# Decoder block on one core: the second half of every block's low parts on GpSimd instead of VectorE

## The chip, the cores and the metric

The kernel runs on one core of a Trainium2 chip. Its engines work side by side, each through its own queue in order: TensorE (PE in the profile, its weight loads PEld), VectorE (DVE), ScalarE (ACT), GpSimd (POOL) and SyncE (SP), which issues the DMAs. They wait for each other through semaphores. The metric is the device time of one execution in microseconds (us), lower is better.

## The reference

One layer of a hybrid decoder over 256 tokens with a width of 2048. It is a chain of matrix products with large weights; everything is float32.

```
h = x + 1/2 * SwiGLU_1(RMSNorm(x))            # gate, up: 2048 x 5632, down: 5632 x 2048
proj = RMSNorm(h) @ W_in                      # 2048 x 7168: q f i g | B C v
o = gated linear recurrence(q, f, i), group norm, * silu(g)      # 8 heads of 128
y = B * causal conv3(C * v), group norm
h = h + concat(o, y) @ W_out                  # 2048 x 2048
h = h + 1/2 * SwiGLU_2(RMSNorm(h))            # as the first
h = h + sigmoid(RMSNorm(h) @ W_pg) * (p @ W_pe)
return RMSNorm(h)
```

## The kernel before, in words

All weights are read once, in blocks: a **step** (class `Step`) is one block of 16 (in every third step of a down projection, 12) square tiles of 128 x 128, and what is done with its product. There are 360 steps: twice 88 for gate and up, twice 48 for down, 72 in the mixer, 16 in the last stage. A token vector is the moving side of the product, 256 tokens wide.

To keep float32 accuracy with the faster float32r products, every operand is split in two: `hi` is the rounded value, `lo` what the rounding left. The activations lie as `xs[:, :T]` (high) and `xs[:, T:]` (low). A tile of weights then needs two matmuls in `product` (lines 104 to 109): `hi` against both halves, 512 columns, and `lo` against the high half, 256 columns.

The weights are split on the chip. `load` brings a block into one of 3 buffers `raw` by a DMA on SyncE's queue (line 85). `split` (line 98) takes a pair of `hi` and `lo` tiles for each half of the block, of 8 tiles or 1024 columns (768 in a block of 12), and calls `split_piece` for each half: ScalarE copies `raw` into `hi` with rounding (line 90), VectorE writes `lo = raw - hi` (line 91). `hi` and `lo` have 4 buffers each, so two blocks are held: the pair for a half of step i + 2 is free once TensorE is done with that half of step i. A `raw` buffer is free for the load of the block three steps on once both its halves are split.

The loop at the end of the kernel asks for the load three steps ahead and the split two steps ahead, then the step's products, its epilogue (VectorE and ScalarE take the sums out of PSUM, scale, gate, and write `hid` or `hT` and `xs`) and hooks, which in the mixer hold the recurrence's own work. A scheduler places the instructions of each engine by its own estimate of when each is ready, so that a queue's order isn't the program's order; only the start of the kernel (line 715 on) is written out by hand. There the first two blocks go side by side while x comes in, steps 2 and 3 are split, and VectorE sums the squares of x (lines 729 and 730) for the first `row_scale` (line 177), whose result the epilogues of the first steps use.

GpSimd does nothing before but fill a few constants: four tiny ones at the start and three memsets (lines 278 and 288) where the mixer opens.

Of the kernel before, what the change touches and what calls it, by code (L numbers as in the profile page):

```python
# [7 lines left out]
F32 = mybir.dt.float32  # L8
F32R = mybir.dt.float32r
I32 = mybir.dt.int32  # L10
AF = mybir.ActivationFunctionType
ALU = mybir.AluOpType
PSUM = bass.MemoryType.PSUM

P = 128
T = 256            # tokens
T2 = 2 * T
NB = 16            # 128-wide blocks of d_model
NF = 44            # 128-wide blocks of d_ff
NH = 8             # heads, conv groups  # L20
EPS = 1e-6
MAGIC = float(0x5F3759DF)
STAGES = (2, 8, 32)  # each joins four blocks of this many tokens
HW = 2 * NH        # heads x windows of 128 tokens
NM = 64 + 192 * len(STAGES)

# columns of the packed per-channel vectors
C_FFN1, C_MIX, C_FFN2, C_PLE, C_FIN = 0, 16, 32, 48, 64
C_HN, C_CN, C_CW, C_LB, C_SEL, C_ID = 80, 81, 89, 113, 129, 139
NCST = C_ID + P  # L30
# [4 lines left out]


class Step:
    """One block of at most 16 x [128, 128] weights and what is done with it."""

    def __init__(self, src, nk, mm, epi=None):  # L40
        self.src, self.nk, self.mm, self.epi = src, nk, mm, epi
# [5 lines left out]
def kernel(  # L47
# [3 lines left out]
    nc = tc.nc  # L51
    V, A, TE = nc.vector, nc.scalar, nc.tensor
# [5 lines left out]

    hT = const.tile([P, NB, T], F32, name="hT")
    xs = const.tile([P, NB, T2], F32R, name="xs")  # L60
    cst = const.tile([P, NCST], F32, name="cst")
    ones = const.tile([P, P], F32, name="ones")
    ones_r = const.tile([P, P], F32R, name="ones_r")
    sel = const.tile([P, 2 * P], F32R, name="sel")
    acc = const.tile([P, T], F32, name="acc")
    rb = const.tile([P, T], F32, name="rb")
    rt = const.tile([P, 2], F32, name="rt")
    lb = const.tile([P, NH], F32, name="lb")
    oml = const.tile([P, NH], F32, name="oml")
    ident = cst[:, C_ID:C_ID + P]  # L70

    def tt(shape=(P, T), dtype=F32, tag="t", bufs=6):
        return tmp.tile(list(shape), dtype, tag=tag, name=tag, bufs=bufs)

# [1 line left out]
    def new_raw(s):  # L76
        s.raw = wpool.tile([P, NB, P], F32, tag="raw", name="raw", bufs=RAW_BUFS)

    def new_parts(s):
        s.half = s.nk // 2  # L80
        s.parts = [tuple(wpool.tile([P, NB // 2, P], F32R, tag=t, name=t) for t in ("hi", "lo"))
                   for _ in range(2)]
# [4 lines left out]
    def split_piece(s, a, b):  # L87
        hi, lo = s.parts[a // s.half]
        r, sl = s.raw[:, a:b, :], slice(a % s.half, a % s.half + b - a)
        A.activation(hi[:, sl, :], r, AF.Copy)  # L90
        V.tensor_tensor(lo[:, sl, :], r, hi[:, sl, :].bitcast(F32), ALU.subtract)  # L91
# [4 lines left out]
            load_piece(s, i * s.nk // n, (i + 1) * s.nk // n)  # L96

    def split(s):
        new_parts(s)
        for k0 in (0, s.half):  # L100
            split_piece(s, k0, k0 + s.half)

    def product(hi, lo, m, ps, first, last):
        """ps[:, :T] += hi.x_hi; ps[:, T:] += hi.x_lo + lo.x_hi"""
        if not first:
            TE.matmul(ps[:, T:], lo, m[:, :T], start=False, stop=False)  # L106
        TE.matmul(ps, hi, m, start=first, stop=last)  # L107
        if first:
            TE.matmul(ps[:, T:], lo, m[:, :T], start=False, stop=False)  # L109

    def product_one(hi, lo, m, ps, first, last):
        """ps[:, :T] += all three"""
        TE.matmul(ps[:, :T], lo, m[:, :T], start=first, stop=False)  # L113
        TE.matmul(ps[:, :T], hi, m[:, T:], start=False, stop=False)  # L114
        TE.matmul(ps[:, :T], hi, m[:, :T], start=False, stop=last)  # L115
# [11 lines left out]
    def new_ps():  # L127
        return psum.tile([P, T2], F32, tag="ps", name="ps")

# [1 line left out]
    def halves(ps):  # L131
        t = tt()
        A.activation(t, ps[:, T:], AF.Copy)  # L133
# [41 lines left out]
    def row_scale():  # L175
        ps = new_ps()
        TE.matmul(ps[:, :T], ones, acc, start=True, stop=True)
        v = tt()
        V.tensor_scalar(v, ps[:, :T], 1.0 / (NB * P), EPS, ALU.mult, ALU.add)
        rsqrt(rb, v)  # L180
# [4 lines left out]
    def token_scale(ps):  # L185
        v = tt(shape=(P, 2), tag="v2", bufs=1)
        for i in range(2):
            V.tensor_scalar(v[:, i:i + 1], ps[i][:, 0:1], 1.0 / (NB * P), EPS, ALU.mult, ALU.add)
        rsqrt(rt, v)
# [11 lines left out]
        prep(j, c_gain)  # L201
        square_sum(j)

# [1 line left out]
    steps = []  # L205

    def at(i, f):
# [14 lines left out]
    def ffn(wg, wu, wd, c_next):  # L222
# [13 lines left out]
        i0 = len(steps)  # L236
        for f in range(NF):
            add(wg[f], NB, *gemm_in(g_epi))
            add(wu[f], NB, *gemm_in(u_epi(f)))

        def open_hid(s):
            st["pool"] = ExitStack()
            pool = st["pool"].enter_context(tc.tile_pool(name="hidp", bufs=1))
            st["hid"] = pool.tile([P, NF, T2], F32R, name="hid")

# [14 lines left out]
        steps[-1].after = close_hid  # L260
        return i0

# [1 line left out]
    def mixer():  # L264
        i0 = len(steps)
        m = {}
# [1 line left out]
        def open_mix(s):  # L268
            st["pool"] = ExitStack()
            m1 = st["pool"].enter_context(tc.tile_pool(name="mix1", bufs=1))  # L270
            m["Y"] = m1.tile([P, NH, T], F32, name="Y")
            m["Q"] = m1.tile([P, NH, T], F32, name="Q")
            m["masks"] = m1.tile([P, NM], F32, name="masks")
# [6 lines left out]
            m2 = st["hg"].enter_context(tc.tile_pool(name="mix2", bufs=1))  # L280
            m["K"] = m2.tile([P, NH, T], F32, name="K")
            m["f"] = m2.tile([P, NH * T], F32, name="f")
            m["t12"] = m2.tile([P, NH * T // 8], F32, name="t12")
            m["tot"] = [m2.tile([P, NH * T // n], F32, name=f"tot{n}") for n in (*STAGES, P)]
            m["V"] = m2.tile([P, 2, NH, P], F32, name="V")
# [49 lines left out]
                V.tensor_tensor(windows(m["Q"][:, h, :]), q_of(h), windows(f), ALU.mult)  # L335
            return epi

        # Tokens are taken in blocks whose length grows. Within a block Q holds q_t times the decays
        # from the block's start through t, K holds k_s times those after s to the block's end, tot
        # the whole block's: a score between two blocks is then a product of rows, no factor of which  # L340
        # exceeds 1, and the blocks between come in with their tot.
        def pairs(a):
            return a.rearrange("p (b two) -> p b two", two=2)

# [55 lines left out]
        def stage_scores(si, h):  # L400
            L = STAGES[si]
            nb = P // (4 * L)
# [44 lines left out]
            return d  # L447

        def stat(key, g, d, first, last):
            """rows g and NH + g: the sum over the group's channels"""  # L450
            if first:
                st[key] = new_ps()
            e = sel[:, P - g:2 * P - g]
            TE.matmul(st[key][:, :T], e, d[:, :T], start=first, stop=False)
            TE.matmul(st[key][:, :T], e, d[:, T:], start=False, stop=last)

        def stat_done(key):
            v = tt()
            V.tensor_scalar(v, st[key][:, :T], 1.0 / P, EPS, ALU.mult, ALU.add)
            r = tt()  # L460
            rsqrt(r, v)
            # rows g hold the high parts, rows NH + g the low ones
            rs = st["rs", key] = m["m1"].tile([P, T], F32R, tag="rs", name="rs", bufs=2)
            A.activation(rs, r, AF.Copy)
            V.tensor_scalar(r, r, cst[:, C_SEL + 9:C_SEL + 10], None, ALU.mult)
            V.scalar_tensor_tensor(rs, rs.bitcast(F32), cst[:, C_SEL + 8:C_SEL + 9], r, ALU.mult, ALU.add)
# [4 lines left out]
            st["nr" + key, g] = d  # L471

        def norm(key, g, t):
            """t (in place) times its group's scale"""
            ps = new_ps()
            TE.matmul(ps[:, :T], ones_r, st["nr" + key, g], start=True, stop=True)
            V.tensor_tensor(t, ps[:, :T], t, ALU.mult)
# [45 lines left out]
        g0 = len(steps)  # L523
# [14 lines left out]
        k = c0 + 3  # L538
# [25 lines left out]
        for h in range(NH):  # L564
            at(k + 2 + h // 2, lambda h=h: norm_rows("o", h))
            at(k + 3 + h // 2, lambda h=h: norm("o", h, m["Q"][:, h, :]))
        assert k + 3 < g0  # a head's norm comes before its gate

        def conv_out(key, c):
            y = m["Y"][:, c, :]  # L570
# [3 lines left out]
        for c in range(NH):  # L574
            key = "y0" if c < 4 else "y1"
# [20 lines left out]
        steps[-1].after = close_mix  # L596
        return i0

# [1 line left out]
    def ple():  # L600
        i0 = len(steps)
        m = st["ple"] = {}
# [84 lines left out]
    scale_at = {i_f1 + 4, i_mix, i_f2, i_ple}  # L687
    late = []

# [1 line left out]
    # the first gate and up blocks side by side, so that both go on while x comes in  # L691
    nc.sync.dma_start(cst, cst_d)
    for i in range(2):
        steps[i].src = w_first[i]
# [17 lines left out]
    with tc.manual_schedule():  # L712
        for a, b in pieces:
            s = steps[a // 8]
# [15 lines left out]
        V.tensor_tensor(acc, acc, rb, ALU.add)  # L730

    def prologue():
        # the lower bound of the forget gate: the softmax's first row
        mx, e0, e1 = (tt(shape=(P, NH), tag="lbt", bufs=3) for _ in range(3))
        l0, l1 = cst[:, C_LB:C_LB + NH], cst[:, C_LB + NH:C_LB + 2 * NH]
        V.tensor_tensor(mx, l0, l1, ALU.max)
        V.tensor_tensor(e0, l0, mx, ALU.subtract)
        V.tensor_tensor(e1, l1, mx, ALU.subtract)
        A.activation(e0, e0, AF.Exp)
        A.activation(e1, e1, AF.Exp)  # L740
        V.tensor_tensor(e1, e0, e1, ALU.add)
        V.reciprocal(e1, e1)
        V.tensor_tensor(lb, e0, e1, ALU.mult)
        V.tensor_scalar(oml, lb, -1.0, 1.0, ALU.mult, ALU.add)
# [23 lines left out]
        if s.after:  # L768
            s.after(s)

# [1 line left out]
    m = st["ple"]  # L772
    ps = st["ts"]
    token_scale(ps)
# [3 lines left out]
    ps = new_ps()  # L778
# [66 lines left out]
```

## Time and profile before

| | |
|---|---|
| time of two runs | 2048.87 and 2050.26 us, median 2049.57 us |
| the profiled execution | span 2047.5 us from first to last instruction; the page gives no other time of its own |
| TensorE (matmuls) | 2028.2 us busy, 99% of the span |
| VectorE | 1373.2 us, 67% |
| ScalarE | 1004.2 us, 49% |
| GpSimd | 2.9 us, 7 instructions |
| DMA | 374 MB read, 184 GB/s over the span |
| chain that ended last | 98% of it matmuls |

The busy share alone doesn't tell what a faster or slower engine would change: the chain of waits tells which engine the end is tied to, the list of waits tells who stands idle for whom, and the timeline shows by how much an instruction is early for the one that needs it.

### The profile page before, as it was taken

The page shows a single profiled execution, that of the slowest core. Times are in us where ns is not written, and L with a number is a line of the kernel's source. Part 1 is how long each engine was busy: PE and PEld are TensorE (multiplying, and loading weights), DVE is VectorE, ACT ScalarE, POOL GpSimd, SP SyncE. Part 2 cuts the span into 40 slices and gives each one's busy share as a digit, 9 for nine tenths or more (in the row PEclk, how much of TensorE's full clock was granted, in tenths as well). Part 3 has the DMA queues.
Part 4 walks back from the last instruction along what each step waited for, and adds up shares of the span by engine and source line. Part 5 has one row for each costly group of instructions (what it writes and reads, how often), then busy time and mean ns, then how long its engine had stood idle before and what let it go on. Part 6 is the DMA issues. An engine that isn't in the chain of part 4 may idle for free.

```text
span 2047.5 us, 29112 instructions
## 1 busy us (share of the span) xinstructions
PE 2028.2 (99%) x11630; PEld 1774.8 (87%) x11630; DVE 1373.2 (67%) x2131; ACT 1004.2 (49%) x1510; POOL 2.9 (0%) x7
## 2 busy tenths in 40 slices
PE   8999999999999999999999999999999999999997
PEld 7888888888888888888888888888888888888986
DVE  8766666666555565689798776666666665555686
ACT  7444444444444444543566544444444444444463
POOL 0000000000000000000000000000000000000000
PEclk9999999999999999999999999999999999999998
DMA  7555555555555555544455555555555555555642
GB/s 250 205 188 188 191 193 188 186 185 182 184 190 190 185 199 190 189 165 145 144 168 186 187 185 192 192 188 185 185 186 187 190 186 188 177 195 187 237 164 84
DMA packets 55720, 378.00 MB, mean 185 GB/s; under 512 B 6176, under 2 KB 6432, under 8 KB 13728
## 3 DMA queue, kind: packets, MB, share of 16 engines
q1 hardware_dynamic: 55584, 376.14, 53.8%
q8 instruction: 91, 1.49, 0.3%
q14 instruction: 45, 0.37, 0.1%
HBM read 374.02 MB, written 2.10 MB: 184 GB/s over the span
## 4 chain that ended last, share of the span: by engine, by line
PE 98%; DMA 1%; DVE 1%; SPq 0%; issue 0%; ACT 0%; DVEq 0%; ACTq 0%
PE ps L107 61%; PE ps L106 29%; PE ps L109 2%; PE ps L405 1%; PE ps L306 1%; PE ps L307 1%; PE ps L308 1%; PE ps L114 1%; PE ps L115 1%; PE ps L113 1%; DMA hT<-xT 0%; DMA raw<-w1g 0%; PE ps L352 0%; DVE hg L782 0%; PE ps L438 0%
## 5 line engine op out<-in xcount | busy, mean ns | idle before, releaser
L107 PE MATMUL ps<-xs,hi 128*128 128x512 f32 x3824 | 1330.7, 394 | 5.9 <-DVE xs L154 5.9
L91 DVE TENSOR_TENSOR lo<-raw,hi 128x1024 fp32r<-128x1024 f32 (+2 forms) x724 | 865.1, 1195 | 637.4 <-ACT hi L90 636.6
L90 ACT ACTIVATE hi<-raw 128x1024 fp32r<-128x1024 f32 (+2 forms) x724 | 750.2, 1037 | 981.3 <-PE ps L107 624.2
L106 PE MATMUL ps<-xs,lo 128*128 128x256 f32 x3585 | 1002.3, 280 | 0.3 <-DVE lo L91 0.3
L107 PEld LDWEIGHTS ps<-xs,hi 128*128 128x128 f32 x3824 | 704.4, 188 | 156.2 <-ACT hi L90 5.9
L106 PEld LDWEIGHTS ps<-xs,lo 128*128 128x128 f32 x3585 | 672.3, 188 | 11.6 <-DVE lo L91 0.8
L107 PE MATMUL ps<-hid,hi 128*128 128x512 f32 x1320 | 461.3, 393 | 0.0
L106 PE MATMUL ps<-hid,lo 128*128 128x256 f32 x1290 | 364.5, 283 | 0.0
L107 PEld LDWEIGHTS ps<-hid,hi 128*128 128x128 f32 x1320 | 245.9, 188 | 54.8
L106 PEld LDWEIGHTS ps<-hid,lo 128*128 128x128 f32 x1290 | 242.5, 188 | 1.5
L140 DVE TENSOR_TENSOR t<-t,rb 128x256 f32<-128x256 f32 x231 | 97.5, 424 | 6.6
L134 DVE TENSOR_TENSOR t<-ps,t 128x256 f32<-128x256 f32 x239 | 99.8, 418 | 0.2 <-ACT t L133 0.2
L133 ACT ACTIVATE t<-ps 128x256 f32<-128x256 f32 x239 | 87.1, 366 | 0.9 <-DVE rb L162 0.9
L107 PE MATMUL ps<-mixout,hi 128*128 128x512 f32 x240 | 83.6, 397 | 0.0
L109 PE MATMUL ps<-xs,lo 128*128 128x256 f32 x239 | 67.8, 284 | 0.1
L106 PE MATMUL ps<-mixout,lo 128*128 128x256 f32 x225 | 63.1, 281 | 0.0
L109 PEld LDWEIGHTS ps<-xs,lo 128*128 128x128 f32 x239 | 45.1, 189 | 10.1 <-DVE lo L91 1.0
L107 PEld LDWEIGHTS ps<-mixout,hi 128*128 128x128 f32 x240 | 44.1, 188 | 9.5
L145 ACT ACTIVATE s<-t 128x256 f32<-128x256 f32 x112 | 45.0, 402 | 0.6 <-DVE t L140 0.6
L106 PEld LDWEIGHTS ps<-mixout,lo 128*128 128x128 f32 x225 | 42.2, 188 | 0.9 <-ACT mixout L149 0.2
L232 DVE TENSOR_TENSOR t<-t 128x256 f32<-128x256 f32 x88 | 37.3, 424 | 2.9
L150 DVE TENSOR_TENSOR hid<-t,hid 128x256 fp32r<-128x256 f32 x88 | 36.7, 418 | 0.1
(177 smaller groups left out, 931.9 us busy)
## 6 DMA issues: line engine op xcount, KB each, us to landing
raw<-w_in SPq DMA_DIRECT2D x48, 1024.0 KB, 4.9
raw<-w2g SPq DMA_DIRECT2D x44, 1024.0 KB, 4.8
raw<-w2u SPq DMA_DIRECT2D x44, 1024.0 KB, 4.8
raw<-w1u SPq DMA_DIRECT2D x43, 1024.0 KB, 4.8
raw<-w1g SPq DMA_DIRECT2D x42, 1024.0 KB, 4.8
raw<-w1d SPq DMA_DIRECT2D x32, 1024.0 KB, 4.9
raw<-w2d SPq DMA_DIRECT2D x32, 1024.0 KB, 4.9
raw<-w_out SPq DMA_DIRECT2D x16, 1024.0 KB, 4.8
```

The costliest lines, as they stand in the source:

```text
L90: A.activation(hi[:, sl, :], r, AF.Copy)
L91: V.tensor_tensor(lo[:, sl, :], r, hi[:, sl, :].bitcast(F32), ALU.subtract)
L106: TE.matmul(ps[:, T:], lo, m[:, :T], start=False, stop=False)
L107: TE.matmul(ps, hi, m, start=first, stop=last)
L109: TE.matmul(ps[:, T:], lo, m[:, :T], start=False, stop=False)
L113: TE.matmul(ps[:, :T], lo, m[:, :T], start=first, stop=False)
L133: A.activation(t, ps[:, T:], AF.Copy)
L134: V.tensor_tensor(t, ps[:, :T], t, ALU.add)
L140: V.tensor_tensor(dst, t, rb, ALU.mult)
L145: A.activation(s, src, AF.Sigmoid)
L150: V.tensor_tensor(dst[:, T:], src, dst[:, :T].bitcast(F32), ALU.subtract)
L232: V.tensor_tensor(u, u, st["g"], ALU.mult)
```

## The change

`split` no longer calls `split_piece` for the second half of a block. ScalarE writes `hi` of that half as before, and the subtraction that writes `lo` is issued on GpSimd, with the same operands and shape. It holds for the 358 blocks that go through `split`; the first two blocks, which are split in pieces by hand, stay as they were. Comment lines were dropped and `split` is longer, so that line numbers behind it are 4 higher than before.

```diff
     def split(s):
+
         new_parts(s)
-        for k0 in (0, s.half):
-            split_piece(s, k0, k0 + s.half)
+        split_piece(s, 0, s.half)
+        hi, lo = s.parts[1]
+        r = s.raw[:, s.half:s.nk, :]
+        A.activation(hi[:, :s.half, :], r, AF.Copy)
+        nc.gpsimd.tensor_tensor(lo[:, :s.half, :], r, hi[:, :s.half, :].bitcast(F32), ALU.subtract)
```

The scheduler answers with other orders. At the start of the kernel, on TensorE, around the matmul that sums the squares over the partitions (`ps<-acc,ones`, of `row_scale`), before:

```order
L107 MATMUL ps<-xs,hi 128x512
L106 MATMUL ps<-xs,lo 128x256
L107 MATMUL ps<-xs,hi 128x512
L177 MATMUL ps<-acc,ones 128x256
L107 MATMUL ps<-xs,hi 128x512
L109 MATMUL ps<-xs,lo 128x256
```

and with the change:

```order
L110 MATMUL ps<-xs,lo 128x256
L111 MATMUL ps<-xs,hi 128x512 x2
L181 MATMUL ps<-acc,ones 128x256
L113 MATMUL ps<-xs,lo 128x256
L110 MATMUL ps<-xs,lo 128x256
L111 MATMUL ps<-xs,hi 128x512
```

Before, it stood at the end of step 4; now it stands behind the first matmul of step 4, 31 matmuls earlier.

On VectorE at the same place, the sums of squares (`acc<-acc,t` and `rb<-rb,t` by turns, then `acc<-acc,rb`) and the low parts around them, before:

```order
L91 TENSOR_TENSOR lo<-raw,hi 128x1024 x4
L729 TENSOR_TENSOR acc<-acc,t 128x256
L729 TENSOR_TENSOR rb<-rb,t 128x256
...
L91 TENSOR_TENSOR lo<-raw,hi 128x1024
L730 TENSOR_TENSOR acc<-acc,rb 128x256
L91 TENSOR_TENSOR lo<-raw,hi 128x1024 x4
L179 TENSOR_SCALAR t<-ps 128x256
```

and with the change:

```order
L91 TENSOR_TENSOR lo<-raw,hi 128x1024 x2
L733 TENSOR_TENSOR acc<-acc,t 128x256
L733 TENSOR_TENSOR rb<-rb,t 128x256
...
L734 TENSOR_TENSOR acc<-acc,rb 128x256
L91 TENSOR_TENSOR lo<-raw,hi 128x1024
L183 TENSOR_SCALAR t<-ps 128x256
```

The low parts of the second halves are gone from VectorE's queue, and that of step 4's first half now stands behind the sum `acc<-acc,rb`.

On GpSimd, where the mixer opens, the memsets stood alone; now they stand among the low parts (`ub` and `S` are tiles of the mixer):

```order
L105 TENSOR_TENSOR lo<-raw,hi 128x768
L105 TENSOR_TENSOR lo<-raw,hi 128x1024
L282 MEMSET ub_6748 128x2
L282 MEMSET ub_6749 128x2
L292 MEMSET S 128x3072
L105 TENSOR_TENSOR lo<-raw,hi 128x1024 x161
```

The low parts behind the memsets wait in the queue until these are done. SyncE's queue holds the same loads in the same order; each now waits for GpSimd as well as for VectorE.

## Rows read from the trace of the kernel before

**Rows 1.** The page: span; busy us by engine; chain that ended last.

```profile
span 2047.5 us, 29112 instructions
...
PE 2028.2 (99%) x11630; PEld 1774.8 (87%) x11630; DVE 1373.2 (67%) x2131; ACT 1004.2 (49%) x1510; POOL 2.9 (0%) x7
...
PE 98%; DMA 1%; DVE 1%; SPq 0%; issue 0%; ACT 0%; DVEq 0%; ACTq 0%
```

**Rows 2.** Waits: who stood idle for whom, total, times, longest in us.

```profile
DVE lo L91 <- ACT hi L90: 636.6, 647, 2.8
...
PE ps L107 <- DVE xs L154: 5.9, 1, 5.9
```

**Rows 3.** Groups by line and shape: count, busy us, mean ns, idle before.

```profile
L91 DVE TENSOR_TENSOR lo<-raw,hi 128x1024 fp32r<-128x1024 f32 x652 | 798.3, 1225 | 581.8 <-ACT hi L90 581.4
L91 DVE TENSOR_TENSOR lo<-raw,hi 128x768 fp32r<-128x768 f32 x64 | 61.3, 958 | 54.6 <-ACT hi L90 54.4
```

**Rows 4.** Timeline, gate and up: start us, us, engine, line, idle before.

```profile
301.09 0.28 PE L109 MATMUL ps<-xs,lo 128*128 128x256 f32 x1
...
301.11 1.06 ACT L90 ACTIVATE hi<-raw 128x1024 fp32r<-128x1024 f32 x1 [1.45 <-PE ps L107]
...
302.21 1.23 DVE L91 TENSOR_TENSOR lo<-raw,hi 128x1024 fp32r<-128x1024 f32 x1 [1.25 <-ACT hi L90]
...
303.46 0.33 SPq L85 DMA_DIRECT2D raw<-w1g  x1
...
303.91 1.06 ACT L90 ACTIVATE hi<-raw 128x1024 fp32r<-128x1024 f32 x1 [1.47 <-issue]
...
306.69 0.28 PE L109 MATMUL ps<-xs,lo 128*128 128x256 f32 x1
```

**Rows 5.** DMA issues: count, KB each, median us from issue to landing.

```profile
raw<-w1u SPq DMA_DIRECT2D x43, 1024.0 KB, 4.8
```

**Rows 6.** Timeline of GpSimd where the mixer opens.

```profile
750.25 2.67 POOL L288 MEMSET S<- 128x3072 f32 x1
```

**Rows 7.** Busy time by stretch: gate and up; the recurrence in the mixer.

```profile
200.00:400.00 200.00, 200.00 (x1143) 174.45 (x1142) 133.77 (x197) 96.51 (x143) 0.00 (x0) 1.00 0.55 187
890.00:985.00 95.00, 94.81 (x559) 85.50 (x558) 90.40 (x196) 41.39 (x56) 0.00 (x0) 1.00 0.43 145
```

**Rows 8.** The same stretches, VectorE's line 91 alone.

```profile
200.00:400.00 200.00, 87.00 (x71) 1.00 0.55 187
890.00:985.00 95.00, 31.27 (x26) 1.00 0.43 145
```

**Rows 9.** Timeline at the start: the split of steps 2 to 4.

```profile
19.11 1.06 ACT L90 ACTIVATE hi<-raw 128x1024 fp32r<-128x1024 f32 x1 [0.21 <-DMA raw<-w1g]
21.59 2.01 ACT L90 ACTIVATE hi<-raw 128x1024 fp32r<-128x1024 f32 x2 [1.42 <-DMA raw<-w1u]
...
28.42 4.13 ACT L90 ACTIVATE hi<-raw 128x1024 fp32r<-128x1024 f32 x4
```

**Rows 10.** Timeline at the start, VectorE: the last sums of squares.

```profile
29.60 0.41 DVE L729 TENSOR_TENSOR rb<-rb,t 128x256 f32<-128x256 f32 x1
...
31.07 0.41 DVE L730 TENSOR_TENSOR acc<-acc,rb 128x256 f32<-128x256 f32 x1
```

**Rows 11.** Timeline at the start, TensorE: steps 2, 4 and 5.

```profile
22.89 0.28 PE L106 MATMUL ps<-xs,lo 128*128 128x256 f32 x1
...
31.07 0.62 PE L107 MATMUL ps<-xs,hi 128*128 128x512 f32 x2
31.53 0.28 PE L109 MATMUL ps<-xs,lo 128*128 128x256 f32 x1
...
36.90 0.59 PE L177 MATMUL ps<-acc,ones 128*128 128x256 f32 x2
37.14 0.58 PE L107 MATMUL ps<-xs,hi 128*128 128x512 f32 x1
```

**Rows 12.** Timeline of the recurrence, TensorE: score products behind VectorE's update `K`.

```profile
963.82 2.84 PE L405 MATMUL ps<-M,K 128*128 128x192 f32 x16 [0.20 <-DVE K L424]
```

## The prediction

> **What bounds the kernel now.** I read the chain that ended last first: 98% of it are matmuls [rows 1], so the end is tied to TensorE and time is won or lost only where TensorE waits. The list of waits comes next: the one long wait of TensorE is 5.9 us, for the first `xs` at the start, while VectorE stands idle for 636.6 us before its low parts [rows 2]. The reader is to see there that the split has time to spare and TensorE, 2028.2 us busy, has not [rows 1]. Last the timeline of one step in gate and up [rows 4]: step to step is 306.69 - 301.09 = 5.60 us, and half a step 2.80 us.
>
> **What is removed.** `split` issues 2 x 358 low parts: 652 of 1024 columns and 64 of 768 [rows 3]. Half of them leave VectorE: 326 x 1.225 + 32 x 0.958 = 430 us of VectorE's time, 21% of the span. On the path that sets the end this is worth nothing. VectorE's low parts had idle time before them nearly everywhere (636.6 us in total [rows 2]), and no matmul of the steady part waits for one. What covers it is TensorE itself, so no gain is booked.
>
> **What is added, and its price.** 358 subtractions on GpSimd. The trace has no GpSimd operation that reads anything. The nearest row is the memset of 3072 columns in 2.67 us [rows 6]: 0.87 ns a column, 0.89 us for 1024 columns, for one stream that is written. That is the lower bound. The subtraction has three streams, two read and one written; one after the other at the memset's rate they take 3 x 0.89 = 2.67 us. I take this value, as it stands on the only row of the same engine. For the upper bound I let each operation also wait out all that VectorE still does in a step: (133.77 - 87.00 / 2) / (200 / 5.60) = 2.53 us [rows 7, 8], so 2.67 + 2.53 = 5.20 us.
>
> [...]
>
> **What covers the new operation in the steady part.** The ScalarE copy at 301.11 starts right as a step ends, so it refills the second half's buffers of the step just done, for use two steps on [rows 4]. The first matmul on that half comes at 306.69 + 2.80 = 309.5. GpSimd can start where VectorE did, at 302.2: it has 7.3 us, and even 5.20 us fits. The second condition is spacing: one such operation a step, so it must take under 5.60 us. The third is the load: SyncE issues the next load at 303.46, as soon as the second half's low part is done [rows 4]. It lands 4.8 us later [rows 5], at 308.3. That buffer belongs to the block three steps on, whose first half is read two steps after the copy at 303.91, at 315.1, so the load may be 6.8 us later. GpSimd delays it by 2.67 - 1.23 = 1.4 us, or 4.0 us at the upper bound. SyncE's queue holds only loads in the same order here, each equally early. ScalarE's queue has nothing that waits for GpSimd. Cost in the steady part: 0 us.
>
> **GpSimd's queue where the mixer opens.** Its low part stands behind the memsets, which wait for the end of the down projection and are done at 750.25 + 2.67 = 752.9 [rows 6]. It is needed a step and a half after that end, about 8.40 us after 750.2, at 758.6. With 2.67 us it is done at 755.6, with 5.20 at 758.1. Cost 0 us.
>
> **The start.** Here the cover is thin. (a) Step 2's second half: its high part is ready at 19.11 + 1.06 = 20.17 [rows 9]; plus 2.67 it is done at 22.84, and TensorE's matmul with it starts at 22.89 [rows 11]. At 5.20 us it would be 2.5 us late. (b) The sum over the partitions moves one step forward, from 36.90 to just behind the pair at 31.07, some 31.3 [rows 11]. Its input is ready when VectorE's sums end: 29.60 + 0.41 = 30.0 [rows 10], then the last addition, 30.4. The low part of step 4's first half now stands behind it and ends at some 31.6; TensorE wants it at 31.53 plus the 37.14 - 36.90 = 0.24 of the moved matmul, 31.77. So there is 0.2 us to spare. GpSimd's operation for step 3 starts at 21.59 + 2.01 = 23.6 [rows 9], just as the sums begin. If it held them up for its whole 2.67 us, TensorE would wait 2.5 us; if that of step 4, ready at about 30.5, did so too, 5.2 us. I take half of the first, 1.3 us, with 0 and 5.2 as ends.
>
> **Sum.** -0 + 0 + 0 + 1.3 us. The profiled execution has a span of 2047.5 us [rows 1]; the runs are 2048.87 and 2050.26 us, 1.4 to 2.8 us lie around the span, and the median is 2.1 us above it. 2047.5 + 2.1 + 1.3 = **2051 us**. The likeliest case alone runs from 2047.5 (no cost, and two microseconds less than the median for orders that happen to fall better) to 2055 (both delays at the start).
>
> **Rival 1: VectorE and GpSimd hold each other up.** A VectorE operation that reads two tiles from SBUF and the new GpSimd one may not run side by side. Against it speaks nothing in the trace, since GpSimd reads nothing there. In gate and up it would still fit: 2.53 + 2.67 = 5.20 of 5.60 us. In the recurrence it wouldn't: VectorE is busy 90.40 of 95 us [rows 7]. It gives away 13 of its 26 low parts, 15.6 us [rows 8], and takes on 13 x 2.67 = 34.7: 109.5 us for 95, 14.5 over. TensorE has nothing to spare there: its score products at 963.82 already waited 0.20 us for the update `K` [rows 12]. With 2.5 to 5.2 us at the start: 2049.6 + 3.9 + 14.5 = 2068 us, between 2055 and 2075. For less speaks that copies out of PSUM and operations with one tile need not be held up.
>
> [...] I keep the forecast ahead, since queues that slip by a microsecond or two find 5 us of cover almost everywhere.
>
> **Rival 2, the other side: GpSimd becomes the bound.** If the spacing of its operations passes 5.60 us, TensorE waits in every step. Alone, an operation would have to take over 5.60 us, 6.3 times the memset's rate; if it is held up by all that VectorE does, over 5.60 - 2.53 = 3.07 us suffice. At 4.0 us, held up: 176 steps of gate and up x 0.93 = 164 us, in the recurrence 14.5 + 13 x 1.33 = 32, at the start 5: 2250 us. The memset's rate speaks against it; that no row shows a subtraction there, speaks for it.
>
> **Rival 3: nothing changes,** because the scheduler leaves the work where it was. The order of GpSimd's queue shows the subtractions there, so I give it next to nothing. Faster by over 2% would need 41 us off a TensorE that is idle for 2047.5 - 2028.2 = 19.3 us in all [rows 1]; the end of the kernel has no split in it.
>
> **Chances.** Forecast 0.63, rival 1 0.21, rival 2 0.14, nothing or a gain 0.02. The range takes the forecast's own range and rival 1 up to its upper end: 2047 to 2075 us, with about 0.81 in it; left out is mainly rival 2. Under 2% either way is about what a measurement here can tell from no change: 41 us. Forecast and rival 1 both lie inside it: same 0.85, slower 0.14, faster 0.01.
>
> **What the profile after should show.** Line 105 on GpSimd x358, near 2.7 us; VectorE some 940 us busy; TensorE's share at 99%, and no long wait for GpSimd's `lo`; small waits, if any, between 20 and 35 us. Rival 1 would show VectorE's operations of two inputs longer than before while GpSimd runs, and waits of the score products in the recurrence. Rival 2 would show GpSimd over 90% busy and TensorE waiting for it in every step. The forecast is wrong if the span moves by more than 8 us, or if the waits at the start are not where the microseconds go.

## The result, and the profile after

The changed kernel takes **2075.3 us** (median of 2073.87 and 2076.72), against 2049.57 before: a ratio of 1.0126, 95% interval 1.0096 to 1.0155. That is 1.3% slower, clear of the noise, though inside the 2% that count as no change. The forecast was 2051 us, the range ended at 2075, and rival 1 stood at 2068.

The page of the kernel after: span, busy us by engine, and the chain that ended last.

```profile
span 2072.1 us, 29503 instructions
...
PE 2037.0 (98%) x11630; PEld 1776.4 (86%) x11630; DVE 1482.1 (72%) x1773; ACT 989.4 (48%) x1510; POOL 866.7 (42%) x365
...
PE 84%; DVE 11%; ACT 3%; issue 2%; DMA 1%; POOL 0%; SPq 0%; DVEq 0%; ACTq 0%; POOLq 0%
```

Against [rows 1] TensorE stands idle for 2072.1 - 2037.0 = 35.1 us instead of 19.3, and the chain now has 11% of VectorE in it. VectorE gave away 430 us of work and is busy for 109 us *more*. So its remaining instructions became longer. The groups of the kernel after, by line and shape (count, busy us, mean ns, idle before), say which:

```profile
L144 DVE TENSOR_TENSOR t<-t,rb 128x256 f32<-128x256 f32 x231 | 424.1, 1837 | 6.9
...
L203 DVE TENSOR_TENSOR t<-hT,t 128x256 f32<-128x256 f32 x45 | 111.4, 2476 | 31.5 <-ACT t L202 31.5
L138 DVE TENSOR_TENSOR t<-ps,t 128x256 f32<-128x256 f32 x239 | 101.1, 423 | 50.7 <-ACT t L137 47.6
...
L105 POOL TENSOR_TENSOR lo<-raw,hi 128x1024 fp32r<-128x1024 f32 x326 | 803.6, 2465 | 1081.5 <-ACT hi L104 1081.5
```

`t<-t,rb` and `t<-hT,t` read two tiles in SBUF. In the kernel before they took 424 and 419 ns:

```profile
L140 DVE TENSOR_TENSOR t<-t,rb 128x256 f32<-128x256 f32 x231 | 97.5, 424 | 6.6
...
L199 DVE TENSOR_TENSOR t<-hT,t 128x256 f32<-128x256 f32 x45 | 18.9, 419 | 0.0
```

Line 138 has the same shape but reads one operand from PSUM, and still takes 423 ns. The low part that stayed on VectorE went from 1225 ns [rows 3] to 1276 only: it runs almost wholly before GpSimd starts. Line 105 is the new operation, 2.47 us.

The waits of the kernel after (total, times, longest in us) show that TensorE waits for GpSimd's low part only a few times, and briefly:

```profile
ACT s L149 <- DVE t L144: 280.7, 109, 4.5
...
PE ps L409 <- DVE K L428: 3.7, 2, 2.0
...
PE ps L113 <- POOL lo L105: 1.5, 7, 0.2
```

ScalarE waits for the long `t<-t,rb` 109 times, 280.7 us in all. TensorE waits for VectorE's update `K` and, 2.7 us in all, for `nr`, an operand of the mixer's norms; it waits seven times for a low part of GpSimd's, all in the output projection (below).

**Where the 24.6 us are,** the difference of the two spans. I set the start of the first weight matmul of a step in a later trace against that of the same step before; the difference is how late the step is. The matmuls of the changed kernel come in the same order as before but for nine. Late, in us:

| step (before at) | what lies behind it | changed kernel | GpSimd writes only | sums in PSUM | only in the mixer | two of 512 columns |
|---|---|---|---|---|---|---|
| 10 (65.38) | the start | 3.27 | 1.32 | 3.49 | -0.02 | 3.78 |
| 160 (885.42) | gate, up, down, mixer's projections | 3.27 | 0.82 | 3.00 | -0.02 | 3.78 |
| 184 (1053.34) | the recurrence, the first norms | 10.16 | 0.41 | 11.25 | 12.01 | 6.82 |
| 200 (1144.41) | the mixer's last norm, the opening of the output projection | 18.32 | 0.58 | 14.88 | 20.09 | 10.63 |
| 209 (1195.39) | the rest of the output projection, one step more | 24.21 | 0.57 | 14.88 | 24.10 | 10.63 |
| 359 (2026.36) | the second feed-forward part, the last stage | 24.21 | 0.58 | 14.88 | 24.10 | 10.63 |

So the changed kernel loses 3.3 us at the start, 6.9 in the recurrence, 8.2 from the last norm to the opening of the output projection, 5.9 from there on, and nothing from step 10 to 160 and from step 209 on. In the recurrence the update `K` itself is no longer than before; operations ahead of it in VectorE's queue are (`M<-Q,tot`, two tiles of SBUF, 1418 ns on the mean instead of 687). (The other columns belong to the experiments below. In those of writing only and of 512 columns, 1.8 and 2.6 us were there already as step 2 opened, before GpSimd's first low part; 0.2 in the changed kernel.)

**Gate and up: held, and yet free.** The timeline of the kernel after (start us, us, engine, line, idle before) at the place of [rows 4]:

```profile
299.92 2.46 POOL L105 TENSOR_TENSOR lo<-raw,hi 128x1024 fp32r<-128x1024 f32 x1 [3.21 <-ACT hi L104]
...
300.60 2.06 DVE L144 TENSOR_TENSOR t<-t,rb 128x256 f32<-128x256 f32 x1
...
302.69 0.42 ACT L149 ACTIVATE s<-t 128x256 f32<-128x256 f32 x1 [2.58 <-DVE t L144]
...
304.38 1.06 ACT L104 ACTIVATE hi<-raw 128x1024 fp32r<-128x1024 f32 x1 [0.33 <-PE ps L111]
...
305.52 2.40 POOL L105 TENSOR_TENSOR lo<-raw,hi 128x1024 fp32r<-128x1024 f32 x1 [3.15 <-ACT hi L104]
```

GpSimd ends at 299.92 + 2.46 = 302.38, VectorE at 300.60 + 2.06 = 302.66, 0.28 us later: it stood until GpSimd was done, then finished. The sigmoid `s` on ScalarE waited 2.58 us for it, and behind the sigmoid in the same queue stands the next copy `hi`, which releases GpSimd's next operation. That is a ring: `hi`, GpSimd, held `t*rb`, sigmoid, next `hi`. Here it still closes in time: the last copy waited 0.33 us for TensorE's release of the buffer (the copy of every second step does), so the ring is shorter than two steps by that much, and the spacing is 305.52 - 299.92 = 5.60 us as before. As the ring keeps pace with the steps, GpSimd's low part is still done some 4.6 us before TensorE comes to the half that needs it.

**Output projection: the same ring, too long.** The timeline of the kernel before, two copies `hi` one step apart:

```profile
1161.53 1.06 ACT L90 ACTIVATE hi<-raw 128x1024 fp32r<-128x1024 f32 x1 [1.01 <-PE ps L107]
...
1167.17 1.06 ACT L90 ACTIVATE hi<-raw 128x1024 fp32r<-128x1024 f32 x1 [1.01 <-PE ps L107]
```

A step takes 1167.17 - 1161.53 = 5.64 us, and the copy waits for TensorE. The kernel after:

```profile
1178.09 1.04 ACT L104 ACTIVATE hi<-raw 128x1024 fp32r<-128x1024 f32 x1
...
1179.21 2.50 POOL L105 TENSOR_TENSOR lo<-raw,hi 128x1024 fp32r<-128x1024 f32 x1 [3.65 <-ACT hi L104]
...
1179.43 2.56 DVE L203 TENSOR_TENSOR t<-hT,t 128x256 f32<-128x256 f32 x1
...
1181.76 0.38 PE L113 MATMUL ps<-mixout,lo 128*128 128x256 f32 x1 [0.23 <-POOL lo L105]
...
1182.56 0.51 ACT L157 ACTIVATE xs<-hT,cst 128x256 fp32r<-128x256 f32 x1 [3.16 <-DVE hT L204]
...
1184.23 1.05 ACT L104 ACTIVATE hi<-raw 128x1024 fp32r<-128x1024 f32 x1
```

From `hi` to `hi` it is 1184.23 - 1178.09 = 6.14 us. The held addition ends 0.28 us behind GpSimd again (1181.99 and 1181.71), and ScalarE stands 3.16 us before `xs`, with no idle time before its copies. So the ring sets 6.14 us, and each of GpSimd's low parts comes 0.5 us later against its step than the one before. The projection also multiplies the second halves of its blocks first (`order`), so that GpSimd's low part is needed as a step opens and not half a step later. Up to step 199 it still comes in time; from step 200 on TensorE waits for it (at 1181.76, just behind GpSimd's end). Seven steps lose 0.5 us each and the last 0.7; the other 1.7 are lost in step 208, the first of the second feed-forward part, where TensorE waits for the last `xs`.

**Norms.** The same view of the kernel after, in the last of the three norms:

```profile
1091.26 2.44 POOL L105 TENSOR_TENSOR lo<-raw,hi 128x1024 fp32r<-128x1024 f32 x1 [4.78 <-ACT hi L104]
...
1091.39 2.58 DVE L470 SCALAR_TENSOR_TENSOR rs<-rs,cst,t 128x256 fp32r<-128x256 f32 x1
...
1094.01 1.31 ACT L474 ACTIVATE nr<-rs,cst 128x256 fp32r<-128x256 f32 x3 [2.56 <-DVE rs L470]
...
1094.57 0.98 PE L480 MATMUL ps<-nr,ones_r 128*128 128x256 f32 x2 [2.42 <-ACT nr L474]
```

A chain of short operations leads from the sum of squares to a matmul. One of them (478 ns before) meets GpSimd and takes 2.58 us, and TensorE waits 2.42. Then the clock falls. Busy time of each engine by stretch in the kernel after; the third number from the right is the granted clock:

```profile
1096.00:1097.00 1.00, 1.00 (x5) 0.90 (x5) 0.57 (x3) 1.00 (x3) 0.00 (x0) 0.50 0.97 410
...
1095.00:1099.00 4.00, 4.00 (x15) 3.53 (x16) 2.91 (x6) 3.56 (x8) 0.70 (x1) 0.57 0.57 231
```

The granted clock is 1.00 elsewhere in the mixer; here, and once more from 1122 to 1126 (mean 0.57 again), it sinks to 0.50. The mean of four microseconds is 0.57: (1 - 0.57) x 4 = 1.7 us lost in each, on top of the waits. Before the first TensorE had stood still for 2.42 us, before the second, where the output projection opens, for 1.28 and then 0.50 us. In the kernel before it stays at 1.00 up to 2034 us, behind the steps.

### The profile page after: what moved, and what is told of

It reads as the page before. It is cut to its first block, busy times and chain, and to the rows that moved or that the text cites. A ratio compares the mean times of both kernels' runs of the same rounds, so it can differ in the third digit from the quotient of the medians.

```text
span 2072.1 us, 29503 instructions
## 1 busy us (share of the span) xinstructions
PE 2037.0 (98%) x11630; PEld 1776.4 (86%) x11630; DVE 1482.1 (72%) x1773; ACT 989.4 (48%) x1510; POOL 866.7 (42%) x365
## 4 chain that ended last, share of the span: by engine, by line
PE 84%; DVE 11%; ACT 3%; issue 2%; DMA 1%; POOL 0%; SPq 0%; DVEq 0%; ACTq 0%; POOLq 0%
PE ps L111 52%; PE ps L110 25%; DVE lo L91 2%; DVE t L203 2%; PE ps L113 1%; ACT hi L90 1%; DVE t L144 1%; PE ps L310 1%; PE ps L311 1%; DVE S L416 1%; PE ps L312 1%; ACT hi L104 1%; PE ps L118 1%; PE ps L119 1%; PE ps L117 1%
## 5 line engine op out<-in xcount | busy, mean ns | idle before, releaser
L105 POOL TENSOR_TENSOR lo<-raw,hi 128x1024 fp32r<-128x1024 f32 x358 | 863.8, 2413 | 1183.5 <-ACT hi L104 1183.5
L91 DVE TENSOR_TENSOR lo<-raw,hi 128x1024 fp32r<-128x1024 f32 (+2 forms) x366 | 452.2, 1236 | 349.3 <-ACT hi L90 348.5
L110 PEld LDWEIGHTS ps<-xs,lo 128*128 128x128 f32 x3585 | 673.0, 188 | 12.5 <-DVE lo L91 1.3
L104 ACT ACTIVATE hi<-raw 128x1024 fp32r<-128x1024 f32 x358 | 371.2, 1037 | 161.3 <-PE ps L111 143.7
L90 ACT ACTIVATE hi<-raw 128x1024 fp32r<-128x1024 f32 (+2 forms) x366 | 373.5, 1020 | 137.0 <-issue 64.3
L144 DVE TENSOR_TENSOR t<-t,rb 128x256 f32<-128x256 f32 x231 | 424.1, 1837 | 6.9
L149 ACT ACTIVATE s<-t 128x256 f32<-128x256 f32 x112 | 46.9, 418 | 280.8 <-DVE t L144 280.7
L153 ACT ACTIVATE hid<-t 128x256 fp32r<-128x256 f32 x88 | 36.7, 417 | 254.6 <-DVE t L236 254.6
L203 DVE TENSOR_TENSOR t<-hT,t 128x256 f32<-128x256 f32 x45 | 111.4, 2476 | 31.5 <-ACT t L202 31.5
L157 ACT ACTIVATE xs<-hT,cst 128x256 fp32r<-128x256 f32 x64 | 31.7, 507 | 141.2 <-DVE hT L204 138.4
L230 DVE TENSOR_TENSOR t<-t,s 128x256 f32<-128x256 f32 x88 | 37.3, 425 | 41.3 <-ACT s L149 41.3
```

Source lines behind the costliest of these rows:

```text
L104: A.activation(hi[:, :s.half, :], r, AF.Copy)
L105: nc.gpsimd.tensor_tensor(lo[:, :s.half, :], r, hi[:, :s.half, :].bitcast(F32), ALU.subtract)
L144: V.tensor_tensor(dst, t, rb, ALU.mult)
L149: A.activation(s, src, AF.Sigmoid)
L203: V.tensor_tensor(t, hT[:, j, :], t, ALU.add)
```

## The experiments

Theory A: VectorE's operations with two SBUF inputs and GpSimd's subtraction exclude each other, and ScalarE's queue passes the delay on. Theory B: the low part is simply ready later. Theory C: the scheduler's other orders cost the time.

**GpSimd writes only.** It subtracts one of the eight tiles and then writes the half twice over, reading nothing; the low parts are left out. TensorE's order is that of the changed kernel; ScalarE's differs from it in 2 of 1510 places, VectorE's in 6 of 1773.

```diff
-        A.activation(hi[:, :s.half, :], r, AF.Copy)
-        nc.gpsimd.tensor_tensor(lo[:, :s.half, :], r, hi[:, :s.half, :].bitcast(F32), ALU.subtract)
+        A.activation(hi[:, :s.half, :], r, AF.Copy); nc.gpsimd.tensor_tensor(lo[:, :1, :], r[:, :1, :], hi[:, :1, :].bitcast(F32), ALU.subtract)
+        for _ in range(2): nc.gpsimd.memset(lo[:, :s.half, :].bitcast(F32), 0.0)
```

> Leaves out the low parts of the second halves: GpSimd subtracts only the first 128 columns of each (which waits for the same high part as before), and two memsets of 1024 columns that read nothing take the place of the rest, so that GpSimd is busy about as long (2 x 0.89 + some 0.4 = 2.2 us against 2.41 us) and the low tile is ready about as late. The orders of TensorE and ScalarE are those of the changed kernel. Theory A (a GpSimd operation that reads SBUF and a VectorE operation with two SBUF inputs exclude each other, and ScalarE's queue passes the delay on to the next high part): VectorE's t*rb back from 1.84 to at most 0.8 us (a hold of 0.4 us is left), time 2049 to 2054 us. Theory B (the low part on GpSimd is simply ready later, 2.41 against 1.23 us, and TensorE waits for it): 2070 to 2076 us. Theory C (the scheduler's other orders, the matmul of the first row scale a step earlier among them, cost by themselves): 2070 to 2076 us.

Measured: 2049.68 us, ratio 0.9999 (0.9989 to 1.0009). The groups of this run:

```profile
L144 DVE TENSOR_TENSOR t<-t,rb 128x256 f32<-128x256 f32 x231 | 97.9, 425 | 6.9
...
L105 POOL MEMSET lo<- 128x1024 f32 x652 | 623.2, 956 | 38.1
L104 POOL TENSOR_TENSOR lo<-raw,hi 128x128 fp32r<-128x128 f32 x358 | 169.4, 473 | 1139.6 <-ACT hi L104 1139.6
```

A mean can be low because the two hardly meet; its timeline shows that they do, a `t*rb` inside the two memsets:

```profile
303.81 1.97 POOL L105 MEMSET lo<- 128x1024 f32 x2
...
303.97 0.43 DVE L144 TENSOR_TENSOR t<-t,rb 128x256 f32<-128x256 f32 x1
```

GpSimd is about as long at work per block (0.47 + 2 x 0.96 = 2.39 us), in almost the same orders, and `t*rb` is back at 425 ns. B and C fall. Low parts on GpSimd aren't late by themselves; it is what GpSimd reads that costs.

**Sums in PSUM.** `t*rb` and `hT+t` get one operand from PSUM, so that they read one tile of SBUF.

```diff
-        t = halves(ps)
+        t = tt(); A.activation(t, ps[:, T:], AF.Copy); V.tensor_tensor(ps[:, :T], ps[:, :T], t, ALU.add)
...
-        V.tensor_tensor(dst, t, rb, ALU.mult)
+        V.tensor_tensor(dst, ps[:, :T], rb, ALU.mult)
...
-        A.activation(t, ps[:, T:], AF.Copy, scale=c)
-        V.tensor_tensor(t, hT[:, j, :], t, ALU.add)
+        A.activation(ps[:, T:], ps[:, T:], AF.Copy, scale=c)
+        V.tensor_tensor(t, hT[:, j, :], ps[:, T:], ALU.add)
```

> The changed kernel, but the sum of the two halves of a product is written back to PSUM before it is multiplied by rb, and the residual's scaled half stays in PSUM too, so that two of VectorE's commonest operations (t*rb and hT+t) have one SBUF input instead of two. GpSimd's work and TensorE's order are unchanged. Theory A: these two go back from 1.84 and 2.48 us to some 0.42 us; the output projection's steps go back from 6.14 to 5.64 us (4.9 us in all); the start (3.3 us) stays, and of the 15 us in the recurrence and the norms some goes: 2058 to 2070 us. Theory B and theory C: unchanged, 2072 to 2077 us.

Measured: 2062.08 us, 1.0062 (1.0047 to 1.0077). Its groups:

```profile
L144 DVE TENSOR_TENSOR t<-ps,rb 128x256 f32<-128x256 f32 x231 | 97.4, 423 | 6.9
L203 DVE TENSOR_TENSOR t<-hT,ps 128x256 f32<-128x256 f32 x45 | 19.0, 421 | 54.1 <-ACT ps L202 54.1
```

Both run through, while GpSimd subtracts as before (one `t*rb` runs from 300.56 to 300.98, inside a subtraction from 299.87 to 302.27). The output projection loses nothing (14.88 late at steps 200 and 209), which is where `hT+t` closed the ring; the recurrence and the start, many of whose two-input operations this leaves alone, lose as much as before or a little more. From the last norm to the opening of the output projection 3.6 us are lost instead of 8.2, with a granted clock of 1.00 there. The same edit in the kernel before:

> A control without GpSimd: the kernel before, with the sums of t*rb and hT+t kept in PSUM. Theory A: nothing is held here, so the edit is worth nothing, 2048.5 to 2051 us, and the 13 us that it gave back in the changed kernel were the held operations. Rival (the edit is a gain by itself, whatever GpSimd does): 2036 to 2046 us.

It took 2051.84 us, 1.0009 (1.0000 to 1.0019): 0.8 us above A's interval. Its trace is 1.7 us late from the recurrence on, so the edit has a small cost of its own there and is no gain. The 13 us that it gave back in the changed kernel came from GpSimd's conflict.

**Outside the mixer and the start only.** GpSimd keeps 278 of the 358 blocks.

```diff
-        nc.gpsimd.tensor_tensor(lo[:, :s.half, :], r, hi[:, :s.half, :].bitcast(F32), ALU.subtract)
+        if s.pool:
+            nc.gpsimd.tensor_tensor(lo[:, :s.half, :], r, hi[:, :s.half, :].bitcast(F32), ALU.subtract)
+        else:
+            V.tensor_tensor(lo[:, :s.half, :], r, hi[:, :s.half, :].bitcast(F32), ALU.subtract)
...
+    for i, s in enumerate(steps): s.pool = i >= 10 and not i_mix <= i < i_f2
```

> GpSimd computes the low parts of the second halves only outside the first 10 steps and outside the mixer (276 of 358 blocks); the rest is VectorE's again. By the lateness of the weight matmuls, gate, up, down and the last stage cost nothing, the start 3.3 and the mixer 20.9 us. Theory A: 2049 to 2052 us, with t*rb still near 2 us in gate and up, hidden. Theory B and C, if the cost were spread over all steps: 19 us x 276/358, 2065 to 2070 us.

Measured: 2050.41 us, 1.0005 (0.9995 to 1.0014), with `t*rb` still held:

```profile
L147 DVE TENSOR_TENSOR t<-t,rb 128x256 f32<-128x256 f32 x231 | 379.5, 1644 | 6.7
```

A held operation costs nothing where the ring has room. **The mixer alone** (`s.pool = i_mix <= i < i_f2`):

> GpSimd takes the second half's low part in the mixer's 72 steps alone; in the other 286 VectorE keeps it. Theory A (the engines exclude each other, and the time is lost only at the start and in the mixer): the changed kernel's 24.2 us of lateness less the 3.3 us of its start, 2049.6 + 20.9 = 2070.5 us, between 2067 and 2074; the start shows no lateness, the output projection again loses some 0.5 us a step. Rival (the losses don't add up: the mixer is late because its queues arrive displaced from the feed-forward part): 2050 to 2060 us.

Measured: 2073.51 us, 1.0114 (1.0099 to 1.0129). The start is clean, as A has it, and the time is in A's interval, but the mixer loses 24.1 us instead of 20.9. The clock tells why. The timeline of TensorE in this run, at the first score products behind an update `K`, and the first of its five stretches at the lower clock:

```profile
943.23 4.48 PE L412 MATMUL ps<-M,K 128*128 128x192 f32 x16 [2.13 <-DVE K L431]
```

```profile
943.00:947.00 4.00, 3.77 (x13) 3.80 (x14) 4.00 (x8) 2.48 (x4) 1.59 (x1) 0.57 0.59 236
```

Right behind a wait of 2.13 us, 16 score products take 4.48 us; 2.84 before [rows 12]. Five such stretches (the others at 987, 1021 and, as in the changed kernel, 1096 and 1124, with means of 0.57 to 0.59) cost some 5 x 1.7 = 8.5 us where the changed kernel has two and 3.4. Without them the mixer's loss is 15.6 and 17.5 us.

**Two instructions of 512 columns** for the one of 1024:

```diff
-        nc.gpsimd.tensor_tensor(lo[:, :s.half, :], r, hi[:, :s.half, :].bitcast(F32), ALU.subtract)
+        for h in (slice(0, s.half // 2), slice(s.half // 2, s.half)):
+            nc.gpsimd.tensor_tensor(lo[:, h, :], r[:, h, :], hi[:, h, :].bitcast(F32), ALU.subtract)
```

> The GpSimd subtraction of 1024 columns goes as two of 512, each about 1.2 us. If a VectorE operation with two SBUF inputs is held until the running GpSimd instruction ends and then goes first: t*rb falls from 1837 ns to some 0.9 to 1.3 us, and the time to 2052 to 2066 us. If GpSimd's next instruction goes ahead of a VectorE operation that already stands waiting: t*rb stays at 1.7 to 2.0 us and the time at 2070 to 2078 us.

Measured: 2060.68 us, 1.0054 (1.0039 to 1.0069). Its groups:

```profile
L145 DVE TENSOR_TENSOR t<-t,rb 128x256 f32<-128x256 f32 x231 | 198.3, 860 | 6.9
...
L106 POOL TENSOR_TENSOR lo<-raw,hi 128x512 fp32r<-128x512 f32 x652 | 906.3, 1412 | 976.3 <-ACT hi L104 974.1 <-DVE mixout L155 2.2
```

VectorE goes between GpSimd's two instructions: in gate and up a pair runs from 300.44 to 303.17, and `t*rb` from 301.13 to 302.02, inside it. The mean of 860 ns is shorter than one of the two, and more than half the loss is gone, with every engine's order that of the changed kernel. From 1030 to 1204 us, where the changed kernel has its two stretches at the lower clock, the granted clock is 1.00.

**Both halves on GpSimd**, the place of rival 2 (low parts of the first half as well):

```diff
-        split_piece(s, 0, s.half)
...
+        for i, (hi, lo) in enumerate(s.parts):
+            r = s.raw[:, i * s.half:(i + 1) * s.half, :]
+            A.activation(hi[:, :s.half, :], r, AF.Copy)
+            nc.gpsimd.tensor_tensor(lo[:, :s.half, :], r, hi[:, :s.half, :].bitcast(F32), ALU.subtract)
```

> GpSimd computes the low parts of both halves: two operations of 2.41 us a step, 4.83 us of 5.60 us; VectorE is left with some 1.3 us a step in gate and up. Theory A: what VectorE reads from SBUF twice (0.8 to 1.3 us a step) has to fit beside 4.83 us, and each hold passes through ScalarE's queue: over 5.60 us a step, 2100 to 2300 us. Theory B: GpSimd's spacing 4.83 us stays under 5.60 us, later low parts cost some tens of us at most: 2075 to 2095 us. Theory C gives no number of its own.

Measured: 2191.22 us, 1.0691 (1.0669 to 1.0712). A wait of TensorE in this run, and ScalarE's and GpSimd's timeline:

```profile
PE ps L112 <- POOL lo L104: 49.0, 100, 3.0
```

```profile
333.27 0.42 ACT L152 ACTIVATE hid<-t 128x256 fp32r<-128x256 f32 x1 [5.03 <-DVE t L235]
...
334.71 10.03 POOL L104 TENSOR_TENSOR lo<-raw,hi 128x1024 fp32r<-128x1024 f32 x4 [1.76 <-ACT hi L103]
```

Now TensorE does wait for GpSimd, 100 times. GpSimd is at work for 80% of the span, so it isn't its own length alone that sets the pace: it idles 1.76 us for `hi`, while ScalarE stood 5.03 us before a held product. At this place it is the ring again, in gate and up as well.

**One tile read, from `raw`.** Is it the reading, or reading two tiles? GpSimd subtracts one tile and multiplies the other seven of `raw` by a constant.

```diff
-        A.activation(hi[:, :s.half, :], r, AF.Copy)
-        nc.gpsimd.tensor_tensor(lo[:, :s.half, :], r, hi[:, :s.half, :].bitcast(F32), ALU.subtract)
+        A.activation(hi[:, :s.half, :], r, AF.Copy); nc.gpsimd.tensor_tensor(lo[:, :1, :], r[:, :1, :], hi[:, :1, :].bitcast(F32), ALU.subtract)
+        nc.gpsimd.tensor_scalar(lo[:, 1:s.half, :], r[:, 1:, :], 0.001, None, ALU.mult)
```

> GpSimd subtracts the first 128 columns alone and then multiplies the other 896 of raw by a constant into lo: one tile read, one written (the low parts are wrong there). Writing alone had held nothing up. If any reading of SBUF by GpSimd holds VectorE's operations of two SBUF inputs: t*rb far above 424 ns, by up to as long as the GpSimd operation itself, and the time above 2053 us wherever that operation is over 1 us. If only a GpSimd instruction that reads two tiles does: t*rb 420 to 600 ns and 2049 to 2052 us.

Measured: 2049.77 us, 1.0000 (0.9991 to 1.0009), `t*rb` 436 ns. By the mean the last branch would hold. The timeline of this run, in gate and up and in the norms, says otherwise:

```profile
302.14 2.46 POOL L105 TENSOR_SCALAR lo<-raw 128x896 fp32r<-128x896 f32 x1 [2.64 <-issue]
...
304.14 0.42 DVE L144 TENSOR_TENSOR t<-t,rb 128x256 f32<-128x256 f32 x1
...
1094.15 3.07 POOL L105 TENSOR_SCALAR lo<-raw 128x896 fp32r<-128x896 f32 x1 [2.18 <-issue]
...
1094.83 1.15 DVE L154 TENSOR_TENSOR mixout<-t,mixout 128x256 fp32r<-128x256 f32 x1
```

The multiplication doesn't read `hi` and doesn't wait for it, so it is nearly over when `t*rb` comes; where VectorE does meet it, as at 1094.83, VectorE takes 1.15 us for 0.42. The mean tells of the place, not of the conflict. So the question was put again, with the operation where the subtraction was.

**One tile read, from `hi`:**

```diff
-        nc.gpsimd.tensor_tensor(lo[:, :s.half, :], r, hi[:, :s.half, :].bitcast(F32), ALU.subtract)
+        nc.gpsimd.tensor_scalar(lo[:, :s.half, :], hi[:, :s.half, :].bitcast(F32), 0.001, None, ALU.mult)
```

> GpSimd multiplies the rounded second half by a constant into lo (the low parts are wrong there): one tile read, one written, 1024 columns, and since it reads hi it starts where the subtraction started, right where t*rb and hT+t come. The queues of TensorE stay as in the changed kernel. If any reading of SBUF by GpSimd holds VectorE's two-input operations to the end of the instruction: t*rb 1.7 to 2.1 us, hT+t some 2.4 us, 2068 to 2078 us. If an instruction that reads one tile lets VectorE in after some 0.7 us (as the few overlapping ones of the run with the multiplication of raw showed: 1.15 us for 0.42): t*rb 0.8 to 1.2 us, hT+t at most 1.3 us, 2050 to 2060 us. If only a GpSimd instruction that reads two tiles holds anything: t*rb 420 to 450 ns, 2049 to 2051 us.

Measured: 2050.33 us, 1.0001 (0.9992 to 1.0011). The groups, and the timeline of gate and up and of the output projection in this run:

```profile
L144 DVE TENSOR_TENSOR t<-t,rb 128x256 f32<-128x256 f32 x231 | 140.9, 611 | 6.9
...
L105 POOL TENSOR_SCALAR lo<-hi 128x1024 fp32r<-128x1024 f32 x326 | 908.5, 2787 | 960.6 <-ACT hi L104 960.6
```

```profile
301.81 2.78 POOL L105 TENSOR_SCALAR lo<-hi 128x1024 fp32r<-128x1024 f32 x1 [2.83 <-ACT hi L104]
302.49 0.63 DVE L144 TENSOR_TENSOR t<-t,rb 128x256 f32<-128x256 f32 x1
...
1156.68 2.78 POOL L105 TENSOR_SCALAR lo<-hi 128x1024 fp32r<-128x1024 f32 x1 [2.87 <-ACT hi L104]
1156.90 1.09 DVE L203 TENSOR_TENSOR t<-hT,t 128x256 f32<-128x256 f32 x1 [0.94 <-ACT t L202]
```

GpSimd's instruction is longer than the subtraction, 2.79 us against 2.47, and yet VectorE is done long before it ends: at 303.12 and 1157.99, 1.31 us behind GpSimd's start both times. Less the 0.28 us of the finish, the hold lasts 1.03 us from GpSimd's start, not 2.78. So the second branch is right in kind and its time at the lower end, though `t*rb` (611 ns) stayed below the 0.8 expected, since it starts 0.68 us into GpSimd's instruction (302.49 - 301.81). This multiplication, which reads one tile, holds VectorE for its first part; the subtraction, which reads two, to its end. The two differ in the operation as well as in the number of tiles, and no run tells which of these makes the difference.

## Why the prediction was wrong

- **Removed: right.** 430 us off VectorE bought nothing. Even where GpSimd does no harm, with 278 blocks moved, the time is that of before.
- **Price: right.** 2.67 us was taken for a subtraction of 1024 columns; unheld ones take 2.40 us, the mean is 2.47.
- **The steady part: 0 us came true in the feed-forward parts and failed in the mixer, by 20.9 us** (24.21 - 3.27 in the table). "ScalarE's queue has nothing that waits for GpSimd" is the sentence that failed. No ScalarE instruction waits for GpSimd's result, but its sigmoid and its `xs` wait for VectorE operations that wait for GpSimd's instruction to end, and the next `hi` stands behind them. In gate and up the cover of the single low part was as forecast, some 4.6 us (7.3 - 2.67), but the ring had only 0.33 us to spare in two steps, and the prediction didn't look at a ring. The output projection, which it let pass under the steady part with the half a step that it gave every second half, had neither and lost 5.9 us.
- **Where the mixer opens: right.** 0 us there: the lateness is 3.27 us at step 10 and at step 160.
- **The start: right place, low value.** 3.3 us against 1.3 taken, inside the bounds of 0 and 5.2. GpSimd's operation for step 3 did hold up the sums of squares:

```profile
23.78 2.50 POOL L105 TENSOR_TENSOR lo<-raw,hi 128x1024 fp32r<-128x1024 f32 x1 [1.05 <-ACT hi L104]
...
24.65 1.91 DVE L733 TENSOR_TENSOR acc<-acc,t 128x256 f32<-128x256 f32 x1 [0.64 <-ACT t L731]
```

  (timeline of the kernel after). The larger piece came later: 1.75 us in step 7, for a low part of VectorE's that its held operations had pushed back.
- **Rival 1: the mechanism that happened, put second.** Its price was 14.5 us for the recurrence and 3.9 for the start. Measured: 6.9 and 3.3. The 14.5 let every VectorE operation exclude every one of GpSimd's, and those from PSUM run through (`t*rb` with one operand there takes 423 ns). The same stretch as [rows 7] in the kernel after:

```profile
890.00:985.00 95.00, 91.31 (x532) 81.94 (x531) 93.45 (x176) 38.69 (x55) 38.79 (x13) 1.00 0.41 139
```

  VectorE is busy 93.45 of 95 us, not 109 for 95. What the sum left out is larger than what it had too much: the last norm and the opening of the output projection (8.2 us, 3.4 of them the clock), and the rest of that projection (5.9). In both no engine is full; what is short is a ring or a chain through three engines, and the prediction looked for full engines only. 2068 and 2075.3 us are near each other by luck, two errors of opposite sign.
- **Its chance: 0.21 was too low.** The prediction saw that nothing in the trace spoke against the rival, and kept its own forecast ahead, since queues that slip "find 5 us of cover almost everywhere". Cover helps against one slip; a ring that is too long takes 0.5 us of it in every step, until nothing is left. The runs show a VectorE operation with two SBUF inputs held by the subtraction to its end (VectorE ends 0.28 us behind it), and not held by writing alone (425 ns). The multiplication, where GpSimd reads one tile, lies between: there the hold ended after 1.03 of 2.78 us, not with the instruction.
- **Rival 2** didn't happen: GpSimd is busy for 42% of the span. Its point of turning exists, as the run with both halves on GpSimd shows.

Not settled: which held operations make the recurrence's 6.9 us. The scheduler's new places cost nothing by themselves: with GpSimd writing only, TensorE's order is that of the changed kernel and VectorE's differs in 6 of 1773 places, and the recurrence loses nothing. But the held operations weren't varied one by one, nor held at their places of before. No version tried beats the kernel before, and with 19.3 us of TensorE's idle time in all there was little to win.

## What to carry to other kernels

Before moving work to GpSimd, list what VectorE does with two SBUF inputs within the new operation's span, lengthen each to GpSimd's end (a subtraction of two tiles held them to 0.28 us behind it here), and follow who waits for it: the ring back to GpSimd's own input must close within one step (6.14 us against 5.64 in the output projection), however idle the engines look. Look also at where a step uses GpSimd's part first. If the move is wanted all the same, cut GpSimd's operation into shorter ones (2060.68 us here, against 2075.3), keep one operand of VectorE's in PSUM (2062.08), or leave the tight stages to VectorE (2050.41). A queue can depend on an engine for whose results it never waits: ScalarE's waited 280.7 us for the held `t*rb`.

## What the runs showed of the hardware

- GpSimd's multiplication of 1024 columns of one tile took 2.79 us, its subtraction of two tiles 2.47, but the multiplication held VectorE for only 1.03 us.
- An int32 operation of VectorE with a single tile as input was held too, which the prediction didn't think of. A group of the kernel after (292 ns before):

```profile
L161 DVE TENSOR_SCALAR rb<-t 128x256 int32<-128x256 int32 x4 | 5.1, 1278 | 0.1
```

  One of the four runs from 1220.64 to 1223.14, beside a subtraction of GpSimd's from 1220.59 to 1222.99, and ends 0.15 us behind it; one that ends before a subtraction starts (1961.55 to 1961.84) takes 0.29 us.

- One wait of TensorE's of 2.13 us cost nearly twice its length in the mixer-only run: the granted clock fell to 0.50 behind it, and the 16 score products took 4.48 us instead of 2.84, another 1.6 us. It isn't always so, and the length alone doesn't decide it: behind the wait of 1.96 us for `K` in the changed kernel's recurrence the granted clock stayed at 1.00. Behind the wait of 1.8 us for `sq` near 1020 us it fell to 0.50 in the mixer-only run (1022 to 1025), and stayed at 1.00 in the changed kernel.
